# Block 0 in pairs of row tiles, and another order of the first loads, in a one-core diffusion layer

## The chip, the cores and the metric

The kernel runs on one core of one Trainium2 chip. The metric is the device time of one execution in microseconds. TensorE (PE, with its weight loads shown apart as PEld) multiplies, VectorE (DVE) and ScalarE (ACT) work on tiles, GpSimd (POOL) helps them, and SyncE (SP) issues most of the loads and stores; ScalarE can issue loads too. Each engine takes its instructions in the order in which they stand, and waits on semaphores for the others.

## The reference

One layer with a context prefix: 1024 latent rows `x` and 256 context rows, of width 1024.

```python
m_lat = sc @ w_mod[l] + b_mod[l]                      # sc = silu(c), six parts of 1024
h_lat = rms_norm(x, norm1_g[l]) * (1.0 + sc1) + sh1
h_ctx = rms_norm(ctx, norm1_g[l]) * (1.0 + csc1) + csh1
y_lat, y_ctx = token_mixers(h_lat, h_ctx, w_in[l], ...)
x = x + g1 * y_lat
h2 = rms_norm(x, norm2_g[l]) * (1.0 + sc2) + sh2
x = x + g2 * conv_ffn(h2, w_up[l], conv_w[l], conv_b[l], w_down[l])
return rms_norm(x, final_g)
```

`token_mixers` projects `h` with `w_in` (1024 x 3584, seven blocks of 512 columns), runs retention and differential attention on it, and projects the result back. The change touches only the first part: shift and scale of the modulation, the norm of the first rows, and their product with the last block of `w_in` (the attention's values).

## The kernel before

Everything is done in tiles of 128. The 1024 latent rows are eight row tiles, `xs0` (tiles 0 to 3, the first half) and `xs1` (4 to 7); the width is eight slices d (or k) of 128 columns. Matrix products take three passes, since each operand is split into a high and a low part: high by high, high by low, low by high (`passes`, L132 to L134). The split of a weight slice is `w_split`: ScalarE writes `whi`, VectorE the rest `wlo`.

Block 0 is the stage at the start, up to the last block of `w_in` for the first rows. Its steps, for each slice d:

- `mod_load(d, q)` loads half q of the modulation weights of slice d (`wt`, 512 KB, five buffers), on SyncE.
- `mod_part(d, q)` multiplies them with the conditioning vector `cz` (`pr`, L522: 4 pieces, 8 matmuls in the trace). `cz` comes from `csil`, the silu of the first columns of `cl`.
- `mod_row(d)` copies the result on ScalarE (`rw`, L526); `mod_sums(d)` adds up four groups of partitions with `fold` on TensorE (`pm`, L532) and writes shift and scale, `mcol`, on VectorE (L533, L534).
- `square`, `power` and `scale` norm a row tile: ScalarE squares, VectorE and GpSimd take the power, VectorE scales.
- `latents(half, d)` turns slice d of four row tiles (`pt`, L550, transposes against `ident`), and `modulate` makes from it the high part `hT[0]` on ScalarE (L553) and the low part `hT[1]` (L555 `tmp`, then L557 on VectorE for even d, on GpSimd for odd d).
- `part_products(ts, k)` adds slice k to the sums of the row tiles ts (`pn`, L596 to L599 for slice 0, L132 to L134 behind it).

`turn_over(n)` writes n products of `ones` by `ones` into a sum that is cleared later; each is two matmuls in the trace (L603).

The order on TensorE, VectorE, ScalarE and SyncE is the order of the program text: `in_order(begin)` links each instruction to the one before it on its engine. The four loads of row tiles 0 to 3 stand ahead of this, on ScalarE, and the load of `ident` on SyncE. A load uses one of eight semaphores in turn, over both queues, so an issue waits until the load eight before it has landed. Behind block 0 come the other six blocks of `w_in`, retention, attention and the gated MLP.

Of the kernel before, what the change touches and what calls it, by code (L numbers as in the profile page):

```python
# [17 lines left out]
P = 128  # L18
D = 1024
# [48 lines left out]
def r32(ap):  # L68
    return ap.bitcast(F32)
# [3 lines left out]
def kernel(  # L73
# [30 lines left out]
    pad(kp, 96)  # L104
    pad(edge, 224)
    ident = kp.tile([P, P], F32, name="ident")
    nc.sync.dma_start(out=ident, in_=consts[:, K_ID : K_ID + P])
# [47 lines left out]
    with ExitStack() as p1:  # L155
# [28 lines left out]
        nc.scalar.activation(csil.rearrange("p k t -> p (k t)"), cl[:, COL_C : COL_C + 16], AF.Silu)  # L184

        def split_slice(src, pool):
            raw = wr.tile([P, 2, 512], F32, name="raw")
# [28 lines left out]
        def lat_lhs(t, k):  # L216
            return tuple(hT[a][t // 4][:, k, (t % 4) * P : (t % 4 + 1) * P] for a in range(2))
# [284 lines left out]
        with ExitStack() as p0:  # L502
            xp = p0.enter_context(tc.tile_pool(name="xp", bufs=1))
            cz = xp.tile([P, KD, 32], F32, name="cz")
            nc.gpsimd.memset(cz, 0.0)
            nc.vector.tensor_copy(cz[:, :, 0:2], csil)
            fold = xp.tile([P, 2], F32, name="fold")
            nc.vector.tensor_tensor(out=fold, in0=ident[:, 0:2], in1=ident[:, 32:34], op=ALU.add)
            for g in (64, 96):
                nc.vector.tensor_tensor(out=fold, in0=fold, in1=ident[:, g : g + 2], op=ALU.add)  # L510
            bsc = xp.tile([P, KD], F32, name="bsc", bufs=7)
            nc.vector.tensor_scalar(out=bsc, in0=cl[:, COL_BMOD + 8 : COL_BMOD + 16], scalar1=1.0, scalar2=None, op0=ALU.add)

            def mod_load(d, q):
                wt = xp.tile([P, 4, 2 * P], F32, name="wt", bufs=5)
                nc.sync.dma_start(out=wt, in_=w_mod[d][:, 4 * q : 4 * q + 4, :])
                wts[d, q] = wt

            def mod_part(d, q):
# [26 lines left out]
            def modulate(tiles, d, who, hi, lo):  # L546
                n = len(tiles) * P
                pt = pst.tile([P, 512], F32, name="pt", tag="tr")
                for i, t in enumerate(tiles):
                    nc.tensor.transpose(pt[:, i * P : (i + 1) * P], t[:, d * P : (d + 1) * P], ident)  # L550
                sh = mcol[:, d, 0, who : who + 1]
                a = mcol[:, d, 1, who : who + 1]
                nc.scalar.activation(hi, pt[:, :n], AF.Identity, scale=a, bias=sh)  # L553
                tmp = xp.tile([P, 512], F32, name="tmp", bufs=2)
                nc.vector.tensor_scalar(out=tmp[:, :n], in0=pt[:, :n], scalar1=a, scalar2=sh, op0=ALU.mult, op1=ALU.add)  # L555
                eng = nc.gpsimd if d % 2 else nc.vector
                eng.tensor_tensor(out=lo, in0=tmp[:, :n], in1=r32(hi), op=ALU.subtract)  # L557
# [6 lines left out]
            def wget(k, c0, c1):  # L564
                return tuple(t[:, k % 2, c0:c1] for t in sl[k // 2])

            def w_load(kk, n=1):
                raws.append(wr.tile([P, 2, 512], F32, name="raw"))
                for i in range(0, 2, 2 // n):
                    nc.sync.dma_start(out=raws[-1][:, i : i + 2 // n], in_=w_in[6][:, 2 * kk + i : 2 * kk + i + 2 // n, :])  # L570

            def w_split(i0=0, i1=2):
                if i0 == 0:
                    sl.append(tuple(wp.tile([P, 2, 512], F32R, name=nm) for nm in ("whi", "wlo")))
                hi, lo = (t[:, i0:i1] for t in sl[-1])
                raw = raws[len(sl) - 1][:, i0:i1]
                nc.scalar.copy(hi, raw)
                nc.vector.tensor_tensor(out=lo, in0=raw, in1=r32(hi), op=ALU.subtract)  # L578

            def load_row(t):  # L580
                nc.sync.dma_start(out=xs1[t - 4], in_=x[t * P : (t + 1) * P, :])

            def latents(half, d):
                modulate((xs0, xs1)[half], d, 0, hT[0][half][:, d, :], hT[1][half][:, d, :])

            def context(d):
                modulate(xc, d, 1, cT[0][:, d, :], cT[1][:, d, :])
# [1 line left out]
            def part_products(ts, k):  # L589
                if k > 0:  # L590
                    for t in ts:
                        passes(part[t], lat_lhs(t, k), wget(k, 0, 512), False, k == KD - 1)
                    return
                hi, lo = wget(k, 0, 512)
                for t in ts:
                    mm(part[t], lat_lhs(t, k)[0], hi, start=True, stop=False)  # L596
# [19 lines left out]
            square(xs0[1], 3)  # L616
            power(2)
            power(3)
            scale(xs0[0], 2)
            square(xs0[2], 4)  # L620
            mod_part(0, 1)
            mod_load(2, 1)
            w_load(1)
            turn_over(2)
            power(4)
            scale(xs0[1], 3)
            square(xs0[3], 5)
            mod_row(0)
            power(5)
            scale(xs0[2], 4)  # L630
            mod_sums(0)
            turn_over(6)
            scale(xs0[3], 5, 0, 2 * P)
            w_split(0, 1)
            latents(0, 0)
            mod_part(1, 0)
            mod_part(1, 1)
            mod_row(1)
            mod_load(3, 0)
            mod_load(3, 1)  # L640
            scale(xs0[3], 5, 2 * P, D)
            w_split(1, 2)
# [971 lines left out]
```

## Time and profile before

| | us |
|---|---|
| median of 3 runs | 1399.6 (1399.48 to 1403.18) |
| the profiled execution | 1400.55 |
| its span | 1398.8 |
| TensorE busy in the span | 1365.4 (98%) |
| VectorE, ScalarE, GpSimd busy | 999.9, 729.8, 297.8 |

The span is the time from the first to the last instruction on the core; the profiled execution has 1.75 us around it. Busy times of engines overlap. Matmuls are pipelined, so a row's duration is longer than the distance from one to the next, and the distance is what counts in a row of them. "Idle before" with an arrow names what ended the wait. Times in the trace are counted from the start of the span.

### The profile page before, as it was taken

How to read it: one execution, taken by the hardware profiler on the slowest of the kernel's cores; microseconds unless marked ns; L12 is line 12 of the kernel's file. 1: busy time of each engine (PE TensorE's matmuls, PEld its weight loads, DVE VectorE, ACT ScalarE, POOL GpSimd, SP SyncE). 2: the span in 40 equal slices, each digit the busy share in tenths (PEclk: the TensorE clock that was granted, in tenths of full speed). 3: DMA queues.
4: the chain of work that ended last, by engine and by line, in shares of the span. 5: the costliest groups of instructions: out<-in, count | busy, mean ns of one | idle time of the engine just before them, and what ended most of it. 6: DMA issues, size and time to landing. Idle time of an engine off the chain costs nothing.

```text
span 1398.8 us, 19411 instructions
## 1 busy us (share of the span) xinstructions
PE 1365.4 (98%) x7024; PEld 1145.6 (82%) x7024; DVE 999.9 (71%) x1458; ACT 729.8 (52%) x1394; POOL 297.8 (21%) x321
## 2 busy tenths in 40 slices
PE   7999999999999999999999999999999999999997
PEld 5788888887887799998878788888888888888885
DVE  3655874424686888886347998887778877798757
ACT  3652322433665699997136655555445555454542
POOL 1310000001656133411201632223332220000001
PEclk9999999999999999999999999999999999999999
DMA  9646885455575697631421223322323225963523
GB/s 329 233 158 207 291 271 179 143 179 168 172 244 157 180 213 167 125 86 58 153 84 60 91 106 114 113 97 106 113 99 113 100 77 174 380 219 105 174 90 128
DMA packets 96807, 218.81 MB, mean 156 GB/s; under 512 B 9220, under 2 KB 31236, under 8 KB 96200
## 3 DMA queue, kind: packets, MB, share of 16 engines
q1 hardware_dynamic: 87832, 190.31, 39.9%
q0 software_dynamic: 8160, 24.91, 7.8%
q10 hardware_dynamic: 720, 2.36, 0.5%
q8 instruction: 55, 0.90, 0.3%
q14 instruction: 40, 0.33, 0.1%
HBM read 160.13 MB, written 57.41 MB: 156 GB/s over the span
## 4 chain that ended last, share of the span: by engine, by line
PE 81%; DVE 6%; DMA 6%; ACT 2%; issue 2%; POOL 1%; SPq 0%; POOLq 0%; ACTq 0%; DVEq 0%
PE chain L132 5%; PE chain L133 5%; PE chain L134 5%; PE pv L876 5%; PE pA L844 5%; PE c L133 4%; PE c L132 4%; PE c L134 4%; PE pn L132 4%; PE pn L134 4%; PE pn L133 4%; PE third L132 3%; PE third L133 3%; PE third L134 3%; PE pl L134 2%; PE pl L133 2%
## 5 line engine op out<-in xcount | busy, mean ns | idle before, releaser
L132 PE MATMUL pl<-hT,whi 128*128 128x512 f32 x256 | 106.2, 415 | 0.0
L132 PE MATMUL chain<-T,whi 128*128 128x512 f32 x264 | 103.2, 391 | 0.7 <-ACT ua L1160 0.4
L133 PE MATMUL chain<-T,whi 128*128 128x512 f32 x264 | 102.8, 389 | 0.0
L134 PE MATMUL chain<-T,wlo 128*128 128x512 f32 x264 | 102.4, 389 | 0.0
L134 PE MATMUL pl<-hT,wlo 128*128 128x512 f32 x256 | 100.3, 392 | 0.3 <-DVE wlo L192 0.3
L133 PE MATMUL pl<-hT,whi 128*128 128x512 f32 x256 | 100.1, 391 | 0.0
L847 DVE TENSOR_REDUCE mt<-pA 128x1 f32<-128x1280 f32 x64 | 95.3, 1490 | 3.5 <-PE pA L844 1.5
L844 PE MATMUL pA<-ks,qhl 128*128 128x512 f32 (+1 forms) x384 | 89.5, 369 | 1.6 <-ACT p L851 1.4
L132 PE MATMUL c<-whi,ghl 128*128 128x512 f32 x232 | 90.2, 389 | 0.0
L133 PE MATMUL c<-wlo,ghl 128*128 128x512 f32 x232 | 90.2, 389 | 0.0
L134 PE MATMUL c<-whi,ghl 128*128 128x512 f32 x232 | 90.2, 389 | 0.0
L851 ACT ACTIVATE p<-pA,mt 128x1280 f32<-128x1280 f32 x64 | 85.5, 1336 | 6.7 <-DVE mt L847 6.7
L1015 ACT CAST whi<-cmb 128x512 fp32r<-128x512 f32 x62 | 38.5, 622 | 81.1 <-PE chain L133 64.0
L844 PEld LDWEIGHTS pA<-ks,qhl 128*128 128x128 f32 x384 | 67.6, 189 | 13.9 <-ACT p L851 2.1
L876 PE MATMUL pv<-va,aT 128*128 128x128 f32 x640 | 77.0, 275 | 0.1
L132 PE MATMUL pn<-whi,hT 128*128 128x512 f32 x188 | 76.8, 408 | 0.0
L876 PEld LDWEIGHTS pv<-va,aT 128*128 128x128 f32 x640 | 74.0, 192 | 0.7 <-DVE yT L905 0.3
L1174 POOL TENSOR_TENSOR cmb<-wrb 128x512 f32<-128x512 f32 x19 | 27.3, 1434 | 221.9 <-DMA wrb<-w_up 157.9
L133 PE MATMUL pn<-wlo,hT 128*128 128x512 f32 x188 | 73.7, 392 | 0.8 <-DVE wlo L578 0.8
L134 PE MATMUL pn<-whi,hT 128*128 128x512 f32 x188 | 73.7, 392 | 0.0
L1018 DVE TENSOR_TENSOR wlo<-cmb,whi 128x512 fp32r<-128x512 f32 x62 | 59.0, 953 | 20.4 <-ACT whi L1015 20.4
L1015 ACT CAST whi<-wra 128x512 fp32r<-128x512 f32 x55 | 33.7, 622 | 74.7 <-PE third L133 42.6
(319 smaller groups left out, 3822.9 us busy)
## 6 DMA issues: line engine op xcount, KB each, us to landing
wm<-w_mod SPq DMA_DIRECT2D x32, 512.0 KB, 5.3
raw<-w_in SPq DMA_DIRECT2D x27, 512.0 KB, 4.4
wra<-w_up SPq DMA_DIRECT2D x24, 512.0 KB, 3.3
wrb<-w_up SPq DMA_DIRECT2D x22, 512.0 KB, 3.5
W<-w_down SPq DMA_DIRECT2D x44, 256.0 KB, 5.8
ad<-s SPq DMA_DIRECT2D x20, 512.0 KB, 3.4
wra<-ad SPq DMA_DIRECT2D x20, 512.0 KB, 3.7
kvs<-kvg SPq DMA_DIRECT2D x36, 256.0 KB, 3.1
```

What stands on the lines that cost most here:

```text
L132: mm(ps, lh, rh, start=first, stop=False, skip_group_check=more)
L133: mm(ps, lh, rl, start=False, stop=False, skip_group_check=more)
L134: mm(ps, ll, rh, start=False, stop=last, skip_group_check=more)
L844: mm(self.pa[m][:, c0:c1], self.q[:, m, i, qs], self.k[:, m, c0:c1], start=(i == 0), stop=(i == 1))
L847: nc.vector.tensor_reduce(out=self.mt[:, m : m + 1], in_=self.pa[m][:, :LK], axis=AX.X, op=ALU.min)
L851: nc.scalar.activation(self.p[m], self.pa[m][:, :LK], AF.Exp, scale=-1.0, bias=self.mt[:, m : m + 1], accum_out=self.s[:, m : m + 1])
L876: mm(self.pv, self.aT[:, c, :], self.v[:, c, :], start=(c == 0), stop=(c == NKT - 1))
L1015: cast = nc.scalar.copy(hi, src)
L1018: nc.vector.tensor_tensor(out=lo, in0=src, in1=r32(hi), op=ALU.subtract)
L1174: nc.gpsimd.tensor_tensor(out=s1, in0=b1, in1=b2, op=ALU.add)
```

## The change

Row tiles 0 and 1 go through slice 0 as a pair, then tiles 2 and 3; the first loads are spread over two queues in another order.

- ScalarE issues the first half of the first modulation weights and row tiles 0 and 1. SyncE issues the rest: the second half, `ident`, half a weight slice, row tiles 2 and 3, the next modulation weights, and so on.
- `latents`, `w_load`, `w_split` take ranges: slice 0 is modulated for tiles 0 and 1, and later for 2 and 3; a weight slice is loaded and split by halves, and its two engines at two places.
- Slice 0's products run pass by pass over a pair of tiles. The two halves of modulation part (1) stand behind the first pair's products, part (2) behind the second pair's.
- Nine `turn_over` products stand at the start, and two, two and six behind: 19 in place of 12.
- Only the columns that slices 0 and 1 need of tiles 1 to 3 are scaled at first, the other 768 later.

```diff
-        for t in range(4):
-            nc.scalar.dma_start(out=xs0[t], in_=x[t * P : (t + 1) * P, :])
...
-            def mod_load(d, q):
+            def mod_load(d, q, eng=nc.sync):
                 wt = xp.tile([P, 4, 2 * P], F32, name="wt", bufs=5)
-                nc.sync.dma_start(out=wt, in_=w_mod[d][:, 4 * q : 4 * q + 4, :])
+                eng.dma_start(out=wt, in_=w_mod[d][:, 4 * q : 4 * q + 4, :])
...
+            def latents(half, d, t0=0, t1=4):
+                modulate((xs0, xs1)[half][t0:t1], d, 0, hT[0][half][:, d, t0 * P : t1 * P], hT[1][half][:, d, t0 * P : t1 * P])
...
                 for t in ts:
                     mm(part[t], lat_lhs(t, k)[0], hi, start=True, stop=False)
+                for t in ts:
                     mm(part[t], lat_lhs(t, k)[0], lo, start=False, stop=False)
-                for t in range(4) if 3 in ts else ():
+                if 3 in ts:
+                    latents(0, 1)
+                for t in ts:
                     mm(part[t], lat_lhs(t, k)[1], hi, start=False, stop=False)
...
-            mod_load(0, 0)
+            mod_load(0, 0, nc.scalar)
+            for t in range(2):
+                load_row(t, nc.scalar)
             mod_load(0, 1)
-            w_load(0, 2)
+            nc.sync.dma_start(out=ident, in_=consts[:, K_ID : K_ID + P])
+            w_load(0, 0, 1)
+            for t in range(2, 4):
+                load_row(t)
             for q in range(2):
                 mod_load(1, q)
+            w_load(0, 1, 2)
             mod_load(2, 0)
-            turn_over(4)
...
+            turn_over(9)
             mod_part(0, 0)
-            square(xs0[0], 2)
-            square(xs0[1], 3)
...
+            mod_load(2, 1)
+            turn_over(2)
             mod_part(0, 1)
...
+            square(xs0[0], 2)
+            power(2)
+            mod_row(0)
+            mod_sums(0)
+            scale(xs0[0], 2)
+            turn_over(6)
+            square(xs0[1], 3)
+            power(3)
+            w_split(0, 1, nc.scalar)
+            scale(xs0[1], 3, 0, 2 * P)
+            w_split(0, 1, nc.vector)
+            square(xs0[2], 4)
             power(4)
-            scale(xs0[1], 3)
+            latents(0, 0, 0, 2)
             square(xs0[3], 5)
...
             for k in range(KD):
                 part_products((0, 1), k)
                 if k == 0:
+                    for q in range(2):
+                        mod_part(1, q)
+                    mod_row(1)
+                    scale(xs0[2], 4, 0, 2 * P)
+                    scale(xs0[3], 5, 0, 2 * P)
+                    latents(0, 0, 2, 4)
                     mod_sums(1)
-                    latents(0, 1)
-                if k < 2:
+                    w_split(1, 2)
+                if k == 1:
+                    mod_sums(2)
+                    latents(0, 2)
                     for q in range(2):
-                        mod_part(k + 2, q)
-                    mod_row(k + 2)
+                        mod_part(3, q)
+                    mod_row(3)
...
                 part_products((2, 3), k)
-                if k + 2 < KD:
+                if k == 0:
+                    for t in range(1, 4):
+                        scale(xs0[t], 2 + t, 2 * P, D)
+                    for q in range(2):
+                        mod_part(2, q)
+                    mod_row(2)
+                if 0 < k < KD - 2:
                     mod_sums(k + 2)
                     latents(0, k + 2)
```

The numbered suffixes in the rows below tell tiles of one name apart: `xs_171` to `xs_174` (before: `xs_172` to `xs_175`) are row tiles 0 to 3, `hT_167` (before `hT_168`) is the high part of the first half, `hT_169` (before `hT_170`) the low part. ScalarE at the start, before and then after:

```order
L179 DMA xs_172<-x 128x1024
L179 DMA xs_173<-x 128x1024
L179 DMA xs_174<-x 128x1024
L179 DMA xs_175<-x 128x1024
L184 ACT_TABLE_LOAD
```

```order
L507 DMA wt<-w_mod 128x1024
L574 DMA xs_171<-x 128x1024
L574 DMA xs_172<-x 128x1024
L615 ACT_TABLE_LOAD
L615 ACTIVATE csil<-cl 128x16
```

One load fewer stands ahead of the table load, and the first is now a half of the modulation weights. SyncE at the start, before and then after:

```order
L98 DMA cl<-cols 128x260
L107 DMA ident<-consts 128x128
L516 DMA wt<-w_mod 128x1024 x2
L570 DMA raw<-w_in 128x512 x2
L516 DMA wt<-w_mod 128x1024 x4
L570 DMA raw<-w_in 128x1024
```

```order
L98 DMA cl<-cols 128x260
L507 DMA wt<-w_mod 128x1024
L607 DMA ident<-consts 128x128
L561 DMA raw<-w_in 128x512
L574 DMA xs_173<-x 128x1024
L574 DMA xs_174<-x 128x1024
L507 DMA wt<-w_mod 128x1024 x2
L561 DMA raw<-w_in 128x512
L507 DMA wt<-w_mod 128x1024 x2
L561 DMA raw<-w_in 128x1024
```

One `wt` stands behind `cl` alone, and row tiles 2 and 3 stand ahead of the weights of slice 1. TensorE from the transposes of slice 0 on, before and then after:

```order
L550 MATMUL pt<-ident,xs_175 128x128
L522 MATMUL pr<-wt,cz 32x256 x8
L596 MATMUL pn<-whi,hT_168 128x512
L597 MATMUL pn<-wlo,hT_168 128x512
L596 MATMUL pn<-whi,hT_168 128x512
L597 MATMUL pn<-wlo,hT_168 128x512
L532 MATMUL pm<-fold,rw 128x2 x2
L550 MATMUL pt<-ident,xs_172 128x128
```

```order
L541 MATMUL pt<-ident,xs_172 128x128
L589 MATMUL pn<-whi,hT_167 128x512 x2
L591 MATMUL pn<-wlo,hT_167 128x512 x2
L595 MATMUL pn<-whi,hT_169 128x512 x2
L513 MATMUL pr<-wt,cz 32x256 x8
L541 MATMUL pt<-ident,xs_173 128x128
L541 MATMUL pt<-ident,xs_174 128x128
L523 MATMUL pm<-fold,rw 128x2 x2
L589 MATMUL pn<-whi,hT_167 128x512 x2
L591 MATMUL pn<-wlo,hT_167 128x512 x2
L541 MATMUL pt<-ident,xs_171 128x128
```

The part of slice 1 (`pr`) moves from ahead of the first products to behind six of them, and the transposes of slice 1 from ahead of the second pair's products into them.

More of the change, by code (lines that the diff above doesn't have):

```diff
@@ L565, in wget, with w_load, w_split @@
                 return tuple(t[:, k % 2, c0:c1] for t in sl[k // 2])
[L567 to L572, printed above, removed]
+            def w_load(kk, i0=0, i1=2):
                 if i0 == 0:
+                    raws.append(wr.tile([P, 2, 512], F32, name="raw"))
+                nc.sync.dma_start(out=raws[-1][:, i0:i1], in_=w_in[6][:, 2 * kk + i0 : 2 * kk + i1, :])
+            def w_split(i0=0, i1=2, only=None):
+                if i0 == 0 and only is not nc.vector:
                     sl.append(tuple(wp.tile([P, 2, 512], F32R, name=nm) for nm in ("whi", "wlo")))
@@ L576, in w_split, with load_row @@
                 raw = raws[len(sl) - 1][:, i0:i1]
[L577 to L584, printed above, removed]
+                if only is not nc.vector:
+                    nc.scalar.copy(hi, raw)
+                if only is not nc.scalar:
+                    nc.vector.tensor_tensor(out=lo, in0=raw, in1=r32(hi), op=ALU.subtract)
+            def load_row(t, eng=nc.sync):
+                eng.dma_start(out=(xs0 + xs1)[t], in_=x[t * P : (t + 1) * P, :])
+            def latents(half, d, t0=0, t1=4):
+                modulate((xs0, xs1)[half][t0:t1], d, 0, hT[0][half][:, d, t0 * P : t1 * P], hT[1][half][:, d, t0 * P : t1 * P])
             def context(d):
@@ L612 @@
             mod_load(2, 0)
-            turn_over(4)
+            nc.scalar.activation(csil.rearrange("p k t -> p (k t)"), cl[:, COL_C : COL_C + 16], AF.Silu)
+            nc.vector.tensor_scalar(out=bsc, in0=cl[:, COL_BMOD + 8 : COL_BMOD + 16], scalar1=1.0, scalar2=None, op0=ALU.add)
+            nc.vector.tensor_copy(cz[:, :, 0:2], csil)
+            turn_over(9)
             mod_part(0, 0)
-            square(xs0[0], 2)
-            square(xs0[1], 3)
-            power(2)
-            power(3)
@@ L619 @@
-            scale(xs0[0], 2)
-            square(xs0[2], 4)
+            mod_load(2, 1)
+            turn_over(2)
             mod_part(0, 1)
-            mod_load(2, 1)
             w_load(1)
             turn_over(2)
+            nc.vector.tensor_tensor(out=fold, in0=ident[:, 0:2], in1=ident[:, 32:34], op=ALU.add)
+            for g in (64, 96):
+                nc.vector.tensor_tensor(out=fold, in0=fold, in1=ident[:, g : g + 2], op=ALU.add)
+            square(xs0[0], 2)
+            power(2)
@@ L666 @@
                 part_products((2, 3), k)
[L667 removed]
+                if k == 0:
+                    for t in range(1, 4):
+                        scale(xs0[t], 2 + t, 2 * P, D)
+                    for q in range(2):
+                        mod_part(2, q)
+                    mod_row(2)
+                if 0 < k < KD - 2:
                     mod_sums(k + 2)
```

22 lines of the change are left out of this document (1 added, 21 removed).

## The prediction

> **What bounds the kernel now.** I read the busy time by stage first, then the chain of waits through the start, then the loads.
>
> ```profile
> 0.00:12.00 12.00, 3.27 (x20) 2.12 (x24) 3.05 (x15) 4.84 (x8) 2.93 (x8) 1.00 0.83 302
> 12.00:31.00 19.00, 19.00 (x127) 13.78 (x128) 9.14 (x19) 6.84 (x12) 2.47 (x3) 1.00 0.93 340
> 100.00:200.00 100.00, 100.00 (x492) 84.36 (x491) 68.53 (x89) 28.25 (x45) 1.92 (x2) 1.00 0.77 258
> ```
>
> Columns: stretch, its length, busy time and count of PE, PEld, DVE, ACT and POOL, granted clock, DMA share, GB/s. PE is the bound from 12 us on (19.00 of 19.00, 100.00 of 100.00) and empty for 8.7 us before. Behind block 0 each engine's order of work is unchanged, so what block 0 gains or loses at its own end moves everything behind it by that much. The chain shows what the start consists of (start, length, what):
>
> ```profile
> 2.12 9.72 DMA wt<-w_mod
> 11.89 1.08 PE pr L522 x8
> 12.97 1.15 PE pn L603 x4
> 14.12 0.86 PE pm L532 x4
> 14.99 2.77 PE pn L603 x12
> 17.76 0.85 PE pt L550 x4
> 18.61 1.87 PE pr L522 x16
> 20.48 0.66 PE pn L596
> ...
> 30.51 0.34 PE pm L532 x4
> 30.85 0.50 PE pt L550 x4
> 31.35 1.00 PE pr L522 x16
> ...
> 35.29 0.34 PE pm L532 x4
> ```
>
> The first useful product (`pn` L596) starts at 20.48, because the second half of the first modulation weights lands only at 11.84. From the sums of slice 3 (`pm` at 30.51) on, before and after give PE the same order: sums, transposes, a modulation part, products. So 30.51 is the yardstick: the question is where the changed kernel has that `pm`.
>
> **The loads.**
>
> ```profile
> GB/s 59 372 343 397 418 416 422 240 273 244 386 341 398 398 411 404 410 386 63 194 191 0 6 191 191 95 0 0 34 101 87 417 407 295 48 53 256 218 194 197
> xs<-x ACTq DMA_DIRECT2D x1, 512.0 KB, 4.2
> cl<-cols SPq DMA_DIRECT2D x1, 130.0 KB, 3.8
> wt<-w_mod SPq DMA_DIRECT2D x1, 512.0 KB, 9.7
> 9.48 1.08 PE L522 MATMUL pr<-wt,cz 128*32 128x256 f32 x8 [6.21 <-DMA wt<-w_mod]
> 9.74 1.06 ACT L538 ACTIVATE sq<-xs 128x1024 bf16<-128x1024 f32 x1 [0.73 <-DMA xs<-x]
> 12.51 1.06 ACT L538 ACTIVATE sq<-xs 128x1024 bf16<-128x1024 f32 x1 [1.62 <-DMA xs<-x]
> ```
>
> The first row is 40 slices of 2.75 us (of the first 110 us): some 0.41 MB per us from 8 us on, summing to 2.1 MB at 8.25 us, 3.2 at 11, 5.5 at 16.5. ScalarE's first load lands 4.2 us after its issue at 0.74, so at 4.94; its third at about 9.7. SyncE's first weights, issued at 1.66 behind `cl` and `ident` (0.72 MB in its queue in all), land at about 9.4, the second at 11.84.
>
> **The change part by part.**
>
> *Queues.* ScalarE now issues w(0,0), row tile 0, row tile 1. By place in the queue they land as the old first, second and third did: 4.94, about 7.6, about 9.7. SyncE issues `cl`, then w(0,1), with 0.66 MB in its queue up to there, issued 0.45 us earlier than the old first weights: the old 7.8 us from issue to landing give 9.0, the bytes give 9.4 − 0.06/0.2 = 9.1. I take 9.1. Bounds: below, 7.9 (a place like ScalarE's second load, whose square began at 7.86); above, 11.84, the old landing. Everything behind on SyncE's queue (row tiles 2, 3, w(1), the second half of the weight slice, w(2), the next slice, w(3)) streams at 0.41 MB/us once ScalarE's queue is empty; counting 1.57 MB on ScalarE and the SyncE bytes, plus the 0.7 us by which `raw` lagged its bytes before, row tile 2 lands at 11.4, tile 3 at 12.7, w(1) at 13.9 and 15.2, the half slice 15.8, w(2) 17.1 and 18.4, the next slice 19.7, w(3) 20.9 and 22.3. SyncE's own waits are these:
>
> ```profile
> SPq L570 <- DMA cl<-cols: 1.4, 1, 1.4
> SPq L516 <- PE pr L522: 16.2, 7, 5.1
> ```
>
> An issue waits for an earlier load to have landed (the load eight before it) and for a weight buffer to be read by PE. Row tile 3 is that one now: it waits for w(0,0), at 4.94, and w(1) and the rest queue behind it. At that time about 1 MB of the 1.5 issued on SyncE is still to come, 2.5 us even at the full rate, so I cost this at nothing; were w(0,0) over 2.5 us late, each further us would count.
>
> *The conditioning vector.* ScalarE's old issue of row tile 3 waited for tile 0, which held the table load and `csil` to 6.8. With three issues `csil` follows `cl` at 4.53, so `cz` is there at 5.2. That is hidden: PE has warm-up products until 5.9.
>
> *PE up to the first product.* Its prices are these rows (start, length, engine, line, operation; the last is a group with its count, busy time and mean in ns):
>
> ```profile
> 1.20 2.08 PE L603 MATMUL pn<-ones 128*128 128x128 f32 x8 [1.20 <-DVE ones L111]
> 13.57 0.35 ACT L526 COPY rw<-pr 128x256 f32<-128x256 f32 x1
> 17.55 1.06 PE L550 MATMUL pt<-ident,xs 128*128 128x128 f32 x4
> 22.03 0.64 PE L550 MATMUL pt<-ident,xs 128*128 128x128 f32 x4
> 9.12 0.75 DVE L544 TENSOR_SCALAR xs<-xs,sm 128x1024 f32<-128x1024 f32 x1
> 15.35 0.35 DVE L544 TENSOR_SCALAR xs<-xs,sm 128x256 f32<-128x256 f32 x1
> 8.10 0.56 POOL L115 TENSOR_TENSOR sm<-sm,mhalf 128x1 f32<-128x1 f32 x1 [7.04 <-DVE sm L114]
> 15.03 0.28 DVE L533 TENSOR_SCALAR mcol<-pm,bsc,cl 128x2 f32<-128x2 f32 x1 [0.50 <-PE pm L532]
> L553 ACT ACTIVATE cT<-pt,mcol 128x256 fp32r<-128x256 f32 x8 | 4.1, 561 | 4.8 <-PE pt L550 4.8
> ```
>
> The same four transposes take 1.06 us at 17.55 and 0.64 at 22.03, and 16 `pr` 1.87 at 18.61 against 1.00 at 31.35, while the granted clock reads 1.00 throughout: PE runs at half pace until some point within those 16 (all at half pace would be 2.16), about 19.6 to 20, and the clock column does not show it. Nine warm-up pairs at 0.52 fill 1.2 to 5.9, part (0,0) 5.9 to 7.0, two more pairs to 8.0. That is 6.8 us without a hole, where before there were 2.1 us and then a hole of 6.2; the old speed-up came after PE had worked from 14.99 on with hardly a hole, some 5 us. I therefore take PE to be at full pace from 8 us on. Half pace to the end is the other bound, priced as a rival.
>
> The Trainium skill, "TensorE: Matmul & The Clock Gate", Part 1, has the array at half rate until a free-running window of about 3.4 us was busy, and back after an idle one. By that rule any start of the window fits one full window into 1.2 to 8.0, and the hole that follows (8.0 to 9.1, at most 6.4 to 9.1) is too short to lose it. The old 5 us agree.
>
> At full pace, from w(0,1) at 9.1: part (0,1) 0.53, copy `rw` with its handover 0.6 → 10.3 (two warm-up pairs lie beneath); `pm` 0.4 → 10.7, `mcol` 0.42 and handover → 11.35. DVE scales row tile 0, 0.75 → 12.1, then adds for the power of tile 1 (its square ran on ACT to 11.4, behind `rw`), 0.15, POOL 0.6 → 12.9, scales 256 columns, 0.35 → 13.3. The six warm-up pairs end at 12.4, beneath. Transposes of tile 1 0.2 with the array's tail 0.2 → 13.7, ACT's eviction at 256 columns 0.56 → 14.35. The first product starts at 14.35 instead of 20.48: **6.1 us earlier**.
>
> *From there to the `pm` of slice 3.* Before, 20.48 to 30.51 is 10.0 us. What is added:
>
> ```profile
> 23.60 0.50 PE L596 MATMUL pn<-whi,hT 128*128 128x512 f32 x1
> 18.65 0.78 ACT L553 ACTIVATE hT<-pt,mcol 128x512 fp32r<-128x512 f32 x1 [4.21 <-PE pt L550]
> 19.46 0.81 DVE L555 TENSOR_SCALAR tmp<-pt,mcol 128x512 f32<-128x512 f32 x1 [3.16 <-ACT hT L553]
> 24.41 1.29 POOL L557 TENSOR_TENSOR hT<-tmp,hT 128x512 fp32r<-128x512 f32 x1 [9.48 <-DVE tmp L555]
> L578 DVE TENSOR_TENSOR wlo<-raw,whi 128x1024 fp32r<-128x1024 f32 x3 | 3.7, 1222 | 0.9 <-ACT whi L577 0.8
> ```
>
> (a) Part (1) lay ahead of the first product; now it lies behind six products: +1.0, from 15.95 to 16.95. (b) Row tiles 2 and 3 get their own transposes, 17.3, and PE waits for their eviction until 18.1 with only `pm` to do: +0.33 and, beside `pm`, 0.3 idle. (c) The transposes of slice 1 now wait for that block's four products, to 19.55. ACT evicts them by 20.5, DVE's `tmp` by 21.4, POOL's low part 1.29 → 22.75. PE has by then done the last products of slice 0, part (2) and two products of slice 1, at 21.7: it stands **1.1 us**, a new wait on POOL, with four products, `pm` and part (3) behind it. Before, the products of tiles 2 and 3 and `pm`, `pt` covered POOL. (d) Small handovers, 0.1. Sum 2.8. Then four products → 23.7, `pm`, `pt` 0.9, part (3) 1.0, six products 1.55: slice 3's `pm` at 27.2. **30.5 − 27.2 = 3.3 us gained.**
>
> The rest costs nothing. DVE's three late scalings (three of about 0.6, one was there before) and the 1.22 us split of the next slice run from 21.4 to 24.3, then `mcol`, ACT, `tmp` and low part for slice 2 end at 27.15; PE needs them at 29.1 to 29.8. Seven extra warm-up pairs lie in the wait for the loads. The loads are wanted later than they land: w(1) at 15.95 and 16.45, w(2) at 20.0, w(3) at 24.6; the closest is 1.2 us, and up to 2 us of delay is free, because POOL's wait covers it. Beyond, each us costs one. Later loads are tied to PE's reads and move with them; before, the queues ran below 280 GB/s from 19 to 27.5, which leaves 1.3 MB, 3 us, to pull them forward.
>
> Reckoned with the same prices, the old order gives 30.6 where the trace has 30.5, so the method is good to some tenths. The profiled execution took 1400.55 us (span 1398.8), 1 us over the median of 1399.6. 1400.55 − 3.3 = 1397.2; against the median I forecast **1396.3 us**, 0.24% less. A change of 0.3% (4.2 us) is about what a measurement of this kernel can tell from none, so this counts as within it, on the faster side.
>
> **The rivals.** *PE still at half pace at the first products.* If holes undo the warm-up and it comes back only between 13.5 and 18.5, part (0,1), the pairs, `pm` and the transposes double: the first product falls at 16 to 17.5 and the gain shrinks to between 1.9 and 0: about 1398.7. For it: 5 us were once needed, and here a hole and several waits cut the work up.
>
> *Slower: the fine waits keep PE cold.* If PE is still at half pace past 18.5, the loss passes the gain: full pace from 21 gives the old yardstick plus 1.5, from 25 on plus 3.2, so 1401 to 1403. Price: the doubled products of slices 0 and 1, with the gain spent from 18.5 on. For it: the half pace at 15 to 18, when PE was full, shows that the speed-up can come late. Against: 6.8 us without a hole at the start.
>
> *The queues do not do what is meant: w(0,1) lands as late as 11.* All loads share the same engines. Beyond 9.1 each us of delay costs one, so 1.9 of 3.3 are lost: 1398.2; past 12.4 nothing is left. Against: the bytes ahead of it are fewer.
>
> The Trainium skill, "DMA: Bandwidth & Descriptors", section "Issuing engines are not separate DMA queues", says that loads from several engines interleave on the same DMA engines and that a second issuer saves only issue time. With an even interleave w(0,1) would land when 1.3 MB have moved, near 6 us, and the sum would be 0.5 better, near 1395.8, since other work then binds. The trace does not agree for SyncE: by it the old first weights (0.72 MB) would have landed near 6.3, and landed at 9.4.
>
> **How the numbers follow.** Forecast 0.62 (own range 1395.2 to 1397.3: w(0,1) from 7.9 to 9.9, handovers, POOL). Half pace to the first products 0.15. Slower through a cold PE 0.10. w(0,1) late 0.08. Loads so early or waits so short that more than 4.2 us come: 0.05 beside the upper tail of the forecast. Range 1394.8 to 1400.4, which leaves out the cold PE and the tail. Faster by over 0.3%: that 0.05 and a fifth to a quarter of the forecast, 0.20; slower by over 0.3% needs 4.2 us, beyond 3.2 for the cold PE, 0.07 with what I have not seen; the same 0.73.
>
> **What would show it.** `wt` waits of PE ending near 5.9 and 9.1; first L589 product near 14.3; four `pt` at 0.6 us near 19; a wait of the L133 product on POOL `hT` of about 1 us near 22; `pm` of slice 3 near 27.2 and the rest of the trace 3.3 us earlier. Wrong would be `pr` at 1.0 us per eight after 9 us, `wt` landing past 10, or PE waiting for `wt` a third time.

## The result, and the profile after

| | before | changed |
|---|---|---|
| median (lowest to highest) of 20 runs each | 1399.86 (1397.37 to 1403.18) | 1396.38 (1393.4 to 1399.43) |
| the profiled execution, its span | 1400.55, 1398.8 | 1398.66, 1396.9 |

The ratio is 0.9974, with a 95% interval of 0.9967 to 0.9981: the changed kernel gains 2.7 to 4.6 us. The forecast was 1396.3 us.

The busy time by stage (columns as in the prediction) for the first two stretches of the changed kernel:

```profile
0.00:12.00 12.00, 8.58 (x58) 7.14 (x59) 2.42 (x15) 4.68 (x8) 1.07 (x6) 1.00 0.83 306
12.00:31.00 19.00, 15.80 (x124) 10.04 (x124) 12.33 (x25) 8.39 (x15) 3.74 (x5) 1.00 1.00 381
```

PE is busy for 8.58 us of the first 12 (3.27 before), most of it warm-up. From 12 to 31 us it now has 3.2 us of idle time where it had none, and yet it is further on at the end: before, 3.9 us of that stretch were warm-up pairs (1.15 and 2.77 in the chain), and the work up to some 19.6 us ran at half pace. The loads keep all DMA engines busy in the second stretch (1.00, 0.93 before).

The chain of waits through the start of the changed kernel (start, length, what):

```profile
2.90 9.84 DMA xs<-x
...
12.82 1.15 ACT sq L529 x2
13.97 0.46 ACT hT L544
...
14.48 0.72 PE pn L589 x2
...
17.75 0.61 PE pm L523 x4
...
20.76 0.82 DVE tmp L546
...
21.65 1.58 POOL hT L548
23.28 0.50 PE pn L133
...
24.47 0.34 PE pm L523 x4
...
27.89 0.34 PE pm L523 x4
...
32.71 0.34 PE pm L523 x4
```

The chain no longer starts at the modulation weights. It starts at row tile 2 (the `xs` load that lands at 12.74), goes through its square on ScalarE and the eviction `hT` queued behind it, and reaches the first product at 14.48 (20.48 before). It ends at POOL's low part of slice 1 and the wait behind it. The sums of slice 3, the yardstick, start at 27.89 (30.51 before), 2.6 us earlier.

The waits of PE in the changed kernel (what waited for what: us in total, times, longest):

```profile
PE pr L513 <- DMA wt<-w_mod: 1.4, 2, 0.8
PE pn L133 <- POOL hT L548: 1.2, 1, 1.2
...
PE pn L589 <- ACT hT L544: 1.1, 1, 1.1
```

The two waits for `wt` (7.5 us in sum before, the longest 6.2) have become two short ones; the two new waits are those of the chain. Some rows of the timeline, all engines (start, length, engine, line, operation, idle time before and what ended it):

```profile
5.98 0.64 PE L513 MATMUL pr<-wt,cz 128*32 128x256 f32 x8 [0.57 <-DMA wt<-w_mod]
...
8.10 0.64 PE L513 MATMUL pr<-wt,cz 128*32 128x256 f32 x8 [0.84 <-DMA wt<-w_mod]
...
8.42 1.06 ACT L529 ACTIVATE sq<-xs 128x1024 bf16<-128x1024 f32 x1 [3.21 <-DMA xs<-x]
...
9.48 0.35 ACT L517 COPY rw<-pr 128x256 f32<-128x256 f32 x1
...
9.69 0.35 DVE L627 TENSOR_TENSOR fold<-fold,ident 128x2 f32<-128x2 f32 x2
...
10.20 0.58 PE L523 MATMUL pm<-fold,rw 128*128 128x2 f32 x4 [0.81 <-DVE sm L113]
...
21.49 2.68 DVE L535 TENSOR_SCALAR xs<-xs,sm 128x768 f32<-128x768 f32 x3
22.02 1.63 DVE L535 TENSOR_SCALAR xs<-xs,sm 128x768 f32<-128x768 f32 x1
```

Eight `pr` take 0.64 us at 5.98 already, where they took 1.08 before: PE is at full pace before the first useful product, and stays there. The last row is the second of the three scalings in the row above it, from a narrower window of the same view.

Does the shift last? The first `pu` product of retention, before and then after:

```profile
276.97 0.67 PE L330 MATMUL pu<-kvs,ks 128*128 128x128 f32 x4
```

```profile
274.27 0.68 PE L326 MATMUL pu<-kvs,ks 128*128 128x128 f32 x4
```

It starts 2.7 us earlier; what block 0 gains arrives there whole. From there to the first attention product `pA` the profiles of this study take between 181.3 and 185.9 us, with the same order of work there. The three longest (185.7 to 185.9: both profiles of the changed kernel, and one of the two of the kernel with the low part on VectorE) are the three in which the granted clock reads 0.91 between 420 and 440 us; in the other eleven it reads 1.00 there and the stretch takes at most 183.5. So one execution's span (1.9 us shorter here) is no measure of a gain of this size. The medians measure its size, and the yardstick shows its place. The kernel before was profiled once, so its 30.51 is of one execution. In the experiments the `pm` of slice 3 is given by the timeline, which puts it at 30.35 before and 27.73 in the changed kernel.

### The profile page after: what moved, and what is told of

It is laid out like the page before. It is cut to its first block, busy times and chain, and to the rows that moved or that the text cites. A ratio compares the mean times of both kernels' runs of the same rounds, so it can differ in the third digit from the quotient of the medians.

```text
span 1396.9 us, 19447 instructions
## 1 busy us (share of the span) xinstructions
PE 1365.7 (98%) x7038; PEld 1146.9 (82%) x7038; DVE 1003.0 (72%) x1462; ACT 729.6 (52%) x1395; POOL 296.9 (21%) x321
## 4 chain that ended last, share of the span: by engine, by line
PE 86%; DMA 5%; DVE 4%; ACT 2%; issue 2%; POOL 1%; SPq 0%; POOLq 0%; ACTq 0%; DVEq 0%
PE chain L131 5%; PE chain L133 5%; PE chain L132 5%; PE pv L893 5%; PE c L132 5%; PE pA L861 5%; PE c L131 5%; PE c L133 5%; PE pn L131 4%; PE pn L133 4%; PE pn L132 4%; PE pl L133 3%; PE pl L131 3%; PE pl L132 3%; PE third L131 3%; PE third L133 3%
```

## The experiments

| kernel | median of runs, us | kernel before beside it | ratio (95%) | first product | `pm` of slice 3 |
|---|---|---|---|---|---|
| loads alone | 1400.94 (12) | 1399.08 (35) | 1.0015 (1.0003 to 1.0028) | 21.70 | 31.54 |
| order alone | 1399.67 (12) | 1399.08 (35) | 1.0009 (0.9999 to 1.0020) | 18.43 | 31.68 |
| one warm-up pair | 1400.31 (11) | 1399.44 (29) | 1.0004 (0.9995 to 1.0014) | 14.33 | 29.82 |
| four first pairs | 1399.86 (12) | 1399.08 (35) | 1.0006 (0.9995 to 1.0017) | 13.90 | 27.15 |
| the same, timed again | 1398.88 (11) | 1399.44 (29) | 0.9996 (0.9988 to 1.0005) | 15.12 | 28.37 |
| one queue | 1394.69 (12) | 1399.08 (35) | 0.9972 (0.9962 to 0.9982) | 13.93 | 28.94 |
| low part on VectorE | 1394.27 (5) | 1400.61 (9) | 0.9962 (0.9949 to 0.9976) | 13.74 | 26.07 |
| the same, timed again | 1396.64 (10) | 1399.44 (29) | 0.9973 (0.9963 to 0.9983) | 14.15 | 26.49 |
| the changed kernel again | 1396.10 (7) | 1399.44 (29) | 0.9970 (0.9960 to 0.9981) | 13.61 | 26.86 |
| all three | 1394.29 (5) | 1400.61 (9) | 0.9953 (0.9938 to 0.9969) | 14.37 | 26.72 |

The last two columns are of one profiled execution each, by the timeline; before, they are 20.41 and 30.35. The changed kernel's `pm` falls at 27.73 in one and 26.86 in another, so differences below 1 us in that column are read from the rows, not from the column.

### The two halves of the change alone

Loads alone: the kernel before, with the changed order of loads. `csil`, `bsc`, `cz` and `fold` move behind the issues that they wait for.

```diff
...
-            mod_load(0, 0)
+            mod_load(0, 0, nc.scalar)
+            for t in range(2):
+                nc.scalar.dma_start(out=xs0[t], in_=x[t * P : (t + 1) * P, :])
             mod_load(0, 1)
-            w_load(0, 2)
+            nc.sync.dma_start(out=ident, in_=consts[:, K_ID : K_ID + P])
...
+            for t in range(2, 4):
+                nc.sync.dma_start(out=xs0[t], in_=x[t * P : (t + 1) * P, :])
             for q in range(2):
                 mod_load(1, q)
...
```

> The kernel before with the changed kernel's loads alone (queues and order of issue); the order of work on the engines stays the old one, so all four row tiles must be scaled before the first transposes. My theory (loads and order of work each bring a part): row tile 3 lands near 14, so the first product starts near 18.4 instead of 20.5, the sums of slice 3 near 28.7 instead of 30.5 (27.9 in the changed kernel), time 1.5 to 2 us under before. Rival, the loads are the whole gain: sums of slice 3 at 27.9, time 3.5 us under before. Rival, the order of work is the whole gain: 30.5, no change.

Order alone: the changed kernel, with the loads as before (row tiles 0 to 3 on ScalarE's queue, the rest on SyncE's).

```diff
-            mod_load(0, 0, nc.scalar)
-            for t in range(2):
+            for t in range(4):
                 load_row(t, nc.scalar)
-            mod_load(0, 1)
             nc.sync.dma_start(out=ident, in_=consts[:, K_ID : K_ID + P])
+            mod_load(0, 0)
+            mod_load(0, 1)
...
```

> The changed kernel with the old loads (four row tiles on ScalarE's queue, the rest on SyncE in the old order). My theory: the second half of the first modulation weights lands at 11.8 again, so the first product starts near 16.6 (14.5 in the changed kernel), the sums of slice 3 near 30.0, time about 0.5 us under before. Rival, the order of work is the whole gain: sums of slice 3 near 27.9, 3.5 us under before.

Loads alone are slower by 0.15%, where a gain of 1.5 to 2 us was expected. The chain of waits of that kernel says why:

```profile
5.71 8.01 DMA xs<-x
...
13.80 1.15 ACT sq L529 x2
14.95 0.27 ACT rw L517
...
15.27 1.01 PE pm L523 x4
16.28 2.77 PE pn L594 x12
```

The second half of the weights was there at 7.95, but in the old order ScalarE copies the modulation (`rw`) behind the squares of all four row tiles, and row tile 3 now comes late. PE stands 5.1 us for that copy and is at half pace behind it (`pm` 1.01, six pairs 2.77).

Order alone gains nothing either, and its `pm` of slice 3 comes 1.3 us later than before, at 31.68. Its timeline of PE:

```profile
1.20 4.21 PE L599 MATMUL pn<-ones 128*128 128x128 f32 x18 [1.20 <-DVE ones L110]
9.63 1.08 PE L513 MATMUL pr<-wt,cz 128*32 128x256 f32 x8 [4.22 <-DMA wt<-w_mod]
...
14.03 0.85 PE L523 MATMUL pm<-fold,rw 128*128 128x2 f32 x4
14.74 2.82 PE L599 MATMUL pn<-ones 128*128 128x128 f32 x12
```

The warm-up pairs run, but PE then stands 4.2 us for the old first weights and starts again at half pace (1.08, and 2.82 for six pairs). The first product starts at 18.43, not at the 16.6 that was expected. From there to the yardstick the new order takes 13.25 us, against 9.94 before (20.41 to 30.35). So it costs 3.3 us behind the first product, and pays only where the first product comes earlier by more than that: by 2.0 us here, by 5.9 in the changed kernel. Neither half brings the gain: the loads bring the weights early, and the order lets ScalarE and PE use them.

### The warm-up

One pair: `turn_over(9)` becomes `turn_over(1)`, and the two, two and six pairs behind it go. These products reach no output.

```diff
-            turn_over(9)
+            turn_over(1)
...
-            turn_over(2)
...
-            turn_over(2)
...
-            turn_over(6)
```

> The changed kernel with one warm-up pair in all instead of nineteen; it leaves out only these products, which reach no output. If TensorE's pace at the start hangs on them: half pace at the first sums (0.9 instead of 0.6) and first products (1.2 instead of 0.7 a pair), full pace not before 17, sums of slice 3 at 29 to 30.5 instead of 27.7, time 1 to 3 us more than the changed kernel. Rival, the loads and the chain over ScalarE and VectorE set the start whatever the pace: sums of slice 3 below 28.2, time as the changed kernel.

Four pairs: only the first group is cut, to the four that the kernel before has.

```diff
-            turn_over(9)
+            turn_over(4)
```

It was profiled three times and timed in two of them; the second profile's single execution took 1398.49 us.

> The changed kernel with four warm-up pairs at the start instead of nine. My theory: with 2.1 us of work and then a hole, TensorE is at half pace until 13 or later; sums, pairs, transposes and first products take double, the sums of slice 3 come at 28.9 to 29.9 instead of 27.9, and 1 to 2 us of the gain are lost. Rival, the loads carry it and the pace at the start does not matter: 27.9, no loss.

> The kernel with four warm-up pairs once more, for another profiled execution. In the first one TensorE was at full pace from 10 us on although the start was short, while the median of its times had lost the gain. If the pace depends on how a window that runs freely falls on the work, executions differ: this one may show half pace at the first sums (about 0.9 us instead of 0.6) and first products (1.2 instead of 0.7), with the sums of slice 3 at 29 or later. Rival, the pace is always as in the first look and the lost time lies elsewhere: sums of slice 3 at 27.3 again.

> Four warm-up pairs at the start, timed a third time, since its two profiles show the gain in full (sums of slice 3 at 27.15 and 26.94) and the median of its times did not. If the profiles are typical: 3 to 4 us under before, like the changed kernel beside it. If executions without the profile often start at half pace: within 1.5 us of before again, with sums of slice 3 still near 27 in the profiled one.

With one pair the first product starts at 14.33, as in the changed kernel, and the time is that of the kernel before (1.0004). Its PE timeline:

```profile
14.33 1.22 PE L589 MATMUL pn<-whi,hT 128*128 128x512 f32 x2 [0.66 <-ACT hT L544]
15.35 1.05 PE L591 MATMUL pn<-wlo,hT 128*128 128x512 f32 x2
...
17.19 1.94 PE L513 MATMUL pr<-wt,cz 128*32 128x256 f32 x16
...
19.62 0.61 PE L523 MATMUL pm<-fold,rw 128*128 128x2 f32 x4
```

Two products take 1.22 us instead of 0.72, and 16 `pr` 1.94 instead of 1.07: PE is at half pace for some 5 us of useful work. That is the half pace of the prediction's rivals, and it leaves 0.5 us of the yardstick's gain. Without the warm-up the change shows no gain in the time.

With four first pairs the profiles differ. In the first and second profile PE is at full pace from 9.9 us on. Six pairs and the transposes of the first profile, and then of the third:

```profile
10.43 1.58 PE L599 MATMUL pn<-ones 128*128 128x128 f32 x12
11.85 0.27 PE L541 MATMUL pt<-ident,xs 128*128 128x128 f32 x1
```

```profile
11.13 2.91 PE L599 MATMUL pn<-ones 128*128 128x128 f32 x12
13.83 0.63 PE L541 MATMUL pt<-ident,xs 128*128 128x128 f32 x2
```

In the third, half pace lasts through the pairs and into the transposes, to about 14, and the first product comes 1.2 us later. The medians of both timings (ratios 1.0006 and 0.9996) show no gain, though two profiles of three show the early yardstick (27.15, 26.94), and the third, at 28.37, is still 2.0 us earlier than before. The twelve times of the first timing fall in two groups, five up to 1398.29 and seven from 1399.62 on, as they would if the pace came late in some; the eleven of the second (1397.43 to 1400.44) show no such gap. How often the pace comes late is not settled by three profiles, and it is not shown that it costs the medians their gain. What the runs show is that with five more pairs the gain is in the median, and without them it is not.

### The queues

All loads on SyncE's queue, in nearly the same order:

```diff
-            mod_load(0, 0, nc.scalar)
-            for t in range(2):
-                load_row(t, nc.scalar)
+            mod_load(0, 0)
             mod_load(0, 1)
             nc.sync.dma_start(out=ident, in_=consts[:, K_ID : K_ID + P])
+            for t in range(2):
+                load_row(t)
```

> The changed kernel with the three ScalarE loads put on SyncE's queue: both halves of the first modulation weights, ident, row tiles 0 and 1, half a weight slice, row tiles 2 and 3, the rest as it was. If all loads share the same engines and only the order counts: first weights land by 5.0 and 6.7, row tile 1 near 9.2, row tile 2 near 11.4, the first product starts near 13.2, the sums of slice 3 near 26.9, time 4 to 4.5 us under before. Rival, the second queue brings speed of its own: the first product later than 14.5, time less than 3.5 us under before.

The ratio is 0.9972, against 0.9974 with two queues. PE's timeline:

```profile
5.46 0.64 PE L513 MATMUL pr<-wt,cz 128*32 128x256 f32 x8 [0.49 <-DMA wt<-w_mod]
...
6.68 0.64 PE L513 MATMUL pr<-wt,cz 128*32 128x256 f32 x8
...
9.55 0.61 PE L523 MATMUL pm<-fold,rw 128*128 128x2 f32 x4 [1.60 <-ACT rw L517]
...
13.93 1.22 PE L589 MATMUL pn<-whi,hT 128*128 128x512 f32 x2 [1.05 <-ACT hT L544]
```

Both halves of the weights are used by 7.3 us (8.10 is the start of the second in the changed kernel). So it is the place in the order that brings the loads early, and no second queue is needed for it. The Trainium skill ("DMA: Bandwidth & Descriptors", "Issuing engines are not separate DMA queues") says that starting loads from several engines at once saves only the time of issuing them; this run agrees. The early weights bring nothing further at once: `rw` waits behind row tile 0's square (8.09 to 9.15), and in this execution PE, after a hole of 1.6 us, fell back to half pace by the first product (1.22). So the first product and the yardstick that were expected (13.2 and 26.9) did not come, while the time did (4.4 us under before between the medians, for 4 to 4.5). Its `pm` of slice 3, at 28.94, is 1.2 us behind that of the changed kernel, and its median is not slower. The two don't fit together unless other executions keep their pace; that stays open.

### The new wait on POOL

The low part of slice 1, which POOL computes, goes to VectorE:

```diff
...
                 if 3 in ts:
-                    latents(0, 1)
+                    latents(0, 1, low=nc.vector)
...
```

> The changed kernel with the low part of slice 1 made on VectorE (0.69 us) instead of GpSimd (1.57 us there). If TensorE's wait of 1.2 us on that part is what gives the start's gain back: the wait falls to 0.3 or less, the sums of slice 3 come at 26.9 instead of 27.9, time about 1 us under the changed kernel (4 to 4.5 under before). Rival, something else is late there (the three late scalings and the split of the next weight slice on VectorE): the wait moves to a later product or transpose and the sums of slice 3 stay at 27.6 or later.

> The low part of slice 1 on VectorE once more, beside the changed kernel in the same call: sums of slice 3 one us before those of the changed kernel, after taking off what row tile 2 lands later or earlier; time 0.5 to 2 us under the changed kernel. Rival, a local gain that later waits take back: no more than 0.3 us under it.

The second of these ran beside the changed kernel itself:

> The changed kernel once more, beside the next three: 3 to 4 us under before, sums of slice 3 at 27.0 to 28.0 (by when row tile 2 lands).

The chain of the first:

```profile
20.02 0.82 DVE tmp L546
20.87 0.70 DVE hT L548
...
21.62 0.50 PE pn L133
...
26.23 0.34 PE pm L523 x4
```

The low part takes 0.70 us in place of 1.58, and PE's wait for it falls from 1.25 to 0.31 us in both profiles. From the first product to the `pm` of slice 3 it is 12.33 and 12.34 us, against 13.25 in both profiles of the changed kernel. So the wait is worth 0.9 us at the yardstick. It is still there at the first `pu` product, 258.5 and 258.6 us behind the first product, against 259.8 and 259.5. In the times it does not stand out: 0.9973 beside 0.9970 on the same chip, where 0.5 to 2 us less were expected, and 0.9962 in the other run, all with overlapping intervals.

This run also shows what the three late scalings cost. In the changed kernel they took 2.68 us from the start of the first to the end of the last; here, with nothing on POOL, they took 1.68 (21.48 to 23.16), each of them 0.62. The whole difference lies in the second one: it started at 22.02, 0.37 us into POOL's low part, took 1.63 us and ended 0.43 us behind that part, while the first and the third took 0.61. The low part on POOL took 1.57 us beside them, 1.29 in the kernel before and 1.30 for the next odd slice of the changed kernel (30.54), with VectorE idle beside both. So the two engines slow each other: for VectorE this run shows it, for POOL the comparison of rows. The Trainium skill, "GPSIMD Engine Reference", section "8. Key points", says that GpSimd shares its interfaces to the on-chip memory with VectorE and contends with VectorE's instructions in a 2-port mode or with two inputs from there. The rows agree that both take longer together; whether the scaling runs in such a mode, none of them shows.

### Row tile 2

The square of row tile 2 behind the first pair's eviction on ScalarE:

```diff
-            square(xs0[2], 4)
-            power(4)
             latents(0, 0, 0, 2)
+            square(xs0[2], 4)
+            power(4)
             square(xs0[3], 5)
```

> The changed kernel with the square of row tile 2 behind the eviction of the first pair on ScalarE. If the eviction is late only because that square stands ahead of it and waits for the row tile: the first product starts at 13.9 instead of 14.5 and the sums of slice 3 come 0.6 earlier, at 27.3. Rival, ScalarE's work on tiles 2 and 3 is what ends last in either order: the first product is earlier, but the second pair's transposes come 0.5 later, and the sums of slice 3 stay between 27.8 and 28.5.

Its chain:

```profile
14.93 1.16 ACT sq L529 x2
...
16.35 0.62 POOL sm L114
...
17.40 0.34 PE pt L541
...
18.38 0.73 PE pn L589 x2
```

The first product comes at 13.91, since the eviction no longer waits for row tile 2. But the squares of tiles 2 and 3 now end at 16.09, so POOL's power and the second pair's transposes come late, and the second pair's products start at 18.38 (18.28 in the changed kernel). The `pm` of slice 3 is at 27.83, and the one profiled execution took 1396.62 us. As its rival had it, what is taken from one pair's wait is put on the other's. ScalarE works without a gap from the eviction at 13.29 to the end of both squares at 16.09, so here its own work binds, and not the landing of row tile 2 (near 12.5).

### All three

One queue, the low part on VectorE, and pairs of warm-up in the two holes that were left (two pairs become seven, and three more stand behind the first transposes):

```diff
-            turn_over(2)
+            turn_over(7)
...
             latents(0, 0, 0, 2)
+            turn_over(3)
             square(xs0[3], 5)
```

> One queue, the low part of slice 1 on VectorE, and warm-up pairs in the holes: seven instead of two behind the second part, three more behind the first transposes. If the half pace in the one-queue run came from its holes (1.6 us before the first sums): the first products at full pace (0.7 instead of 1.2 us a pair) from 13.9 on, the sums of slice 3 near 26.3 (29.1 with one queue alone), time 4.5 to 5.5 us under before. Rival, pairs do not hold the pace, or stand in the way: sums of slice 3 at 27.5 or later, time as with one queue alone (4 us under before) or worse.

This has the lowest ratio of all, 0.9953 (0.9938 to 0.9969), but its interval overlaps that of the changed kernel, and its median (1394.29) is that of the low part alone beside it (1394.27), so the queue and the pairs add nothing that these five runs each can show. With the first hole down to 0.46 us PE keeps its full pace in this execution (0.73 for two products at 14.37), which fits the reading that the holes cost the one-queue kernel its pace. Its waits of PE, and then its chain:

```profile
PE pr L513 <- DMA wt<-w_mod: 1.6, 2, 0.9
```

```profile
9.92 11.00 DMA wt<-w_mod
...
24.90 8.86 DMA wt<-w_mod
...
33.80 0.64 PE pr L513 x8
```

Of these two waits the first ends at 6.05, at the very start, and the second at 33.80, behind the yardstick, where it takes 0.7 us of the gain. The chain shows one more: the weights that land at 20.92 hold up the sixteen `pr` of part (2), which take 1.40 us for 1.07. So the loads bind twice behind the first product, and the margin that the prediction counted on, weights that land before they are wanted, is used up. That is as far as reordering block 0 went here.

## Why the prediction was right, and which steps were not

**The size and the sign.** Forecast 3.3 us, measured 3.5 between the medians (2.7 to 4.6 by the interval). The yardstick moved by 2.6 in the profiled execution and by 3.5 in the second one (30.35 to 26.86). Forecast of the yardstick 27.2; the chain has 27.89. The prediction took 4.2 us as about the least that a measurement can tell from none; with 20 runs each the interval is 1 us to either side. That the sum comes this near is in part luck, since errors of a microsecond in it cancel, as the next points show.

**Queues.** w(0,1) was used from 8.10, not from 9.1. w(0,0) was forecast to land at 4.94, a microsecond before it was wanted; the nine pairs ended at 5.41, not 5.9, and PE waited 0.57 us for it, to 5.98. The early second half brought nothing, since two other things stood there: row tile 0 landed at 8.4, not 7.6, so that its square on ScalarE ran ahead of the copy `rw` until 9.48; and `fold`, which waits for `ident`, ended at 10.04. The step "part (0,1), copy `rw`, `pm`" was worked out as if ScalarE were free, and without `ident`. Both errors are near 1 us and cancel by luck: `pm` at 10.20, forecast 10.3.

**Pace.** Full pace was taken from 8 us on; it was there at 5.98 (in the second profile of the kernel with the low part on VectorE, with the same start, only from 6.9), and no later work fell back. The runs with fewer pairs bear out that the pairs bring the pace. The reason given, that some 5 us of unbroken work bring it, they do not bear out. The prediction counted these 5 us from 14.99 on, but in its own chain PE works without a hole from 11.89 on, nearly 8 us before the pace comes. In the third profile with four pairs PE worked without a hole from 5.94 to 13.8 at half pace, in the first one only from 5.61 to 9.9. What decides within these bounds stays open, so here the forecast was better than its reason.

**First product.** 14.48 for 14.35, but by another way. The transposes ended 0.3 us earlier than worked out, while row tile 2 landed at 12.74 and not at 11.4. Its square stands ahead of the first pair's eviction on ScalarE, and the prediction didn't name what is queued behind it. In the second profile, with row tile 2 there by 11.8, the first product started at 13.61. So the start moves by up to 0.9 us between executions of one kernel, and this landing goes with it.

**(a) and (b).** Part (1) 1.0 us, as forecast; the second pair's products start 3.8 us behind the first product, 3.75 forecast.

**(c).** The wait on POOL is there, 1.25 us for 1.1. But the low part was priced at 1.29 from a row beside which VectorE was idle (24.34 to 26.08), and took 1.57. The miss of 0.7 us at the yardstick consists of 0.18 up to `tmp`, 0.30 for POOL, and 0.29 for the four products behind the wait (1.24 us from POOL's end, for 0.95: the first after a wait takes 0.50, not 0.23), less 0.08 in the rest.

**"The rest costs nothing."** For PE that held: no third wait for `wt`, and VectorE's split of the next slice came in time. The three scalings, though, were taken as 0.6 us each off the path, at no cost. Two of them took that, the second took 1.63, and it is they that stood beside POOL's low part, which is on the path. That they cost nothing is the step that failed: beside them POOL's part took 0.3 us longer than the row it was priced from.

**The rivals.** Half pace at the first products was not what happened with nine pairs. The kernel with one pair was at half pace to about 19 us, between the first rival and the second, and there the gain is gone from the time (1.0004), as the prediction reckoned for 18.5. The late weights did not come, nor did half pace past 18.5.

**Even interleave.** The prediction cites the Trainium skill ("DMA: Bandwidth & Descriptors", "Issuing engines are not separate DMA queues") for loads from several engines that interleave, with a second issuer saving only issue time. By an even interleave it had w(0,1) land near 6, and set that aside, since the trace of before did not agree. With the two queues it was 8.10, between 6 and the 9.1 of the forecast; with one queue both halves were in use by 7.3. That a second issuer saves little held for this kernel (0.9972 and 0.9974), and which of the two landings was right did not matter, because other work bound by then.

## What to carry to other kernels

An early load pays only if every engine that handles it has it next in its order: the loads alone were slower here (1.0015), because one copy stood behind four squares. Where PE waits for the start of a kernel, price its pace too: the same order of work without warm-up products showed no gain. And a step that is moved is priced with what runs beside it at its new place: POOL's part and the scalings put next to it cost more together than either row had shown.

## What the hardware showed beside this

- The clock column reads 1.00 in both stretches of the changed kernel and in those of the kernel before, while six pairs take 1.58 or 2.91 us. The pace has to be read from repeated rows of one shape.
- PE was back at half pace by 11.65 in the one-queue kernel, after a hole of 1.6 us and 1.8 us of pairs behind it; after holes of 0.8 and 1.1 us in the changed kernel it was not.
- One kernel (four first pairs) reached full pace near 9.9 us in two executions and near 14 us in a third, at the same order of work and nearly the same landings (second `pr` at 7.84 and 8.11).
- The landing of row tile 2 in the changed kernel was 12.8 us in one execution and 11.8 us in another.
- VectorE's 768-column scaling took 0.61 or 0.62 us, and 1.63 us when it started within POOL's low part; that part took 1.29 us with VectorE idle and 1.57 us beside the scalings.
- The granted clock read 0.91 between 420 and 440 us in three of fourteen profiled executions, the three that were slowest from the first `pu` to the first `pA`.
